# Indexer scores in fewer, fuller visits of tiled products, with five scratch banks and three main banks

## The chip, the cores and the metric

The kernel runs on one core of a Trainium2 chip. The metric is the device time of one execution in microseconds (us), taken as the median of several runs. The engines that matter here are TensorE (PE in the profile, with its weight loads as PEld), VectorE (DVE), ScalarE (ACT), GpSimd (POOL) and SyncE (SP), which issues the DMAs. Products land in PSUM banks; DVE and ACT read them from there.

## The reference, cut to what matters

Two layers act on a prompt of 256 tokens and on eight sample requests of 16 tokens, which the kernel keeps side by side as 384 columns. In each layer, one projection of the normalised input yields queries, keys, values, indexer queries and keys, head weights, gates and the inputs of a convolution and of a pooling branch. The indexer decides which keys each query may attend to:

```python
logits = jnp.einsum('bqhd,bsd->bqhs', qi, ki) * IDX_DIM ** -0.5
score = jnp.einsum('bqhs,bqh->bqs', jax.nn.relu(logits), wi) * N_IDX_HEADS ** -0.5
score = jnp.where(visible[None], score, -jnp.inf)
_, idx = lax.top_k(score, topk)
```

There are 16 indexer heads of width 64. For the prompt, the kernel computes the scores of queries 0 to 63 not at all (all their keys are taken), of queries 64 to 127 over 128 keys, and of queries 128 to 255 over 256 keys; for each sample request it computes them over 144 keys. The rest of a layer is softmax attention over the chosen keys, a depthwise convolution with layer norm, windowed pooling, gates, the output projection, and a gated embedding term.

## The kernel before

**Products of inputs with weights.** `mstep` computes 128 output rows of a projection for all 384 tokens. It takes a bank of PSUM with the tag "mm", runs 16 blocks of depth 128 and, for each, three products in fp32r: high part by high part (L238), low part of the input by high part of the weight (L239), and high by low (L240). That is 48 products with 384 columns, in two halves of 24. The weights come in pieces of eight blocks. SP loads a piece into one of three raw buffers, ACT rounds it to its high part `whi` (L114), and DVE subtracts to get the low part `wlo` (L115). The reading of a finished bank, called its evacuation here, isn't issued at the end of a step: it is put into a queue, and `run_pending` issues it in the middle of the next step.

**Side work.** The indexer, the softmax, the convolution, the pooling and the norm's statistics lie in generators (`att_gen` is that of the attention). After each half step `pump` advances one of them to its next `yield`, so that the side work's products stand between the halves of the main products. They use PSUM banks with the tag "sd". Both tags have four banks of the eight.

**The steps around the change.** The steps of a layer run in the order t0, gb0, ga0, qi0 to qi7, gb1, ga1, v, four pooling steps, k0, k1, gb2, ga2, q0 to q3, gb3, ga3, q4 to q7, and three kinds of gate steps. The step t0 yields the indexer's keys and the head weights. Its evacuation `ev_t0` (L387 to L395) first scales the tables (L347) by the row scale `rb`, and then makes `wiT` (L387, DVE) and the keys (L390 DVE, L391 and L392 ACT, and so on). `rb` comes out of the statistics: small products at L156, a reciprocal and a root (L161 to L166), three transposes on PE (L170), and a copy (L175). The steps qi0 to qi7 leave out the first 64 tokens and so have 320 columns.

**The indexer.** `att_gen` waits until t0 has been evacuated, transposes the head weights (L627) and spreads those of the sample requests (L629). Once the qi steps are done it computes the scores of the first 128 keys and then of all 256 in eight visits each. A visit takes two "sd" banks and has two products (L651), one for each of two heads, which lie in the upper and the lower 64 rows of the array. ACT applies the relu, and DVE weighs each head and adds (L658, L660). `topk` follows (L609 and L612, on DVE). For the sample requests there are eight such pairs (L691), each followed by a weighing on DVE (L696, L698) and a sum over heads on PE (L680). Every product of the indexer in plain fp32 shows as two records, so a pair shows as "x4".

**What sets the order.** The program goes through a scheduling framework that fixes each engine's order of instructions at build time. It places a step when its buffers are free by its own plan, so the number of banks moves instructions.

Of the kernel before, what the change touches and what calls it, by code (L numbers as in the profile page):

```python
# [47 lines left out]
def hybrid_kernel(ctx, tc, I, O):  # L48
# [99 lines left out]
    def bank(tag):  # L148
        return psum.tile([128, 512], F32, name=tag, tag=tag, bufs=4)

# [82 lines left out]
    def run_pending(gate):  # L233
        while pending and gate():
            pending.popleft()()
# [92 lines left out]
    for l in range(DEPTH):  # L328
# [4 lines left out]
        with ExitStack() as mixctx:  # L333
            mix = mixctx.enter_context(tc.tile_pool(name=f"mix{l}", bufs=1))

            def mt(shape, tag, bufs=1, dt=F32, name=None):
                return mix.tile(list(shape), dt, name=name or tag, tag=tag, bufs=bufs)
# [42 lines left out]
            wiT = mt([16, N], "gth", name="wiT")  # L380
            wi_tok = mt([128, 2, 16], "wi_tok")
            wi_s = mt([128, 2, NB], "wi_s")
# [238 lines left out]
            def att_gen():  # L621
                while "t0" not in flags:
                    yield

                ps = bank("sd")
                for i in range(2):
                    T.transpose(ps[:, 16 * i:16 * i + 16], wiT[:, 128 * i:128 * i + 128], ident[0:16, 0:16])  # L627
                for j in range(2):
                    T.matmul(ps[:, 128 + 128 * j:256 + 128 * j], em[0:16, 128 * j:128 * j + 128], wiT[:, TP:],  # L629
                             start=True, stop=True)  # L630
                V.tensor_copy(wi_tok.rearrange("p a b -> p (a b)"), ps[:, 0:32])
                w2 = mt([128, 2, 128], "rp", bufs=2, name="w2")
# [4 lines left out]
                while "qi" not in flags:  # L637
                    yield


                for qt in range(2):
                    nk = 128 * (qt + 1)
                    r = slice(64, 128) if qt == 0 else slice(0, 128)
                    c = slice(0, 64) if qt == 0 else slice(64, 192)
                    acc = mt([128, TP], "sc", bufs=2)[r, :nk]
                    for t in range(8):

                        pss = [bank("sd") for _ in range(2)]
                        for j in range(2):
                            h = slice(64 * j, 64 * j + 64)  # L650
                            T.matmul(pss[j][r, :nk], qi[t][h, c], kiT[h, :nk], start=True, stop=True)  # L651
                        rl = mt([128, 512], "rp", bufs=2, name="rl")[r]
                        for j in range(2):
                            A.activation(rl[:, j * nk:j * nk + nk], pss[j][r, :nk], AF.Relu)
                        for j in range(2):
                            w = wi_tok[r, qt, 2 * t + j:2 * t + j + 1]
                            if t == 0 and j == 0:
                                V.tensor_scalar(acc, rl[:, :nk], w, None, OP.mult)  # L658
                            else:
                                V.scalar_tensor_tensor(acc, rl[:, j * nk:j * nk + nk], w, acc, OP.mult, OP.add)  # L660
                        yield
                    if qt == 0:
                        G.memset(maskp[0][0:64, 0:64], 0.0)
                        G.memset(maskp[0][0:64, 64:128], OFF)
                    else:
                        V.memset(acc[0:64, nk - 64:nk], NEG)
                    yield from topk(acc, 64)
                    V.tensor_scalar(maskp[qt][r], acc, TAKEN, OFF, OP.not_equal, OP.mult)
                    yield

                scp = bank("sd")

                def load_ki(b):
                    kb = mt([128, 2, KS], "kb", bufs=2, name="kib")[:, 0, :]
# [7 lines left out]

                kb = load_ki(0)
                yield
                before = None
                for b in range(NB):
                    nxt = load_ki(b + 1) if b + 1 < NB else None
                    pss = [bank("sd") for _ in range(2)]
                    for j in range(2):
# [4 lines left out]
                    rl = mt([128, 512], "rp", bufs=2, name="rls")  # L694
                    for j in range(2):
                        V.tensor_scalar(rl[:, j * KS:j * KS + KS], pss[j][:, :KS], 0.0,  # L696
                                        wi_s[:, j, b:b + 1], OP.max, OP.mult)
                    V.tensor_tensor(rl[:, :KS], rl[:, :KS], rl[:, KS:2 * KS], OP.add)  # L698
                    before, kb = rl, nxt
                    yield  # L700
                add_s(NB - 1, before)
                flags.add("idx")
# [438 lines left out]
```

## Time and profile before

| what | value |
|---|---|
| median of three runs | 1517.2 us (1515.77 to 1517.27) |
| the profiled execution's own time | 1517.27 us |
| its span, first to last instruction | 1515.4 us |
| PE busy | 1493.7 us, 99% |
| DVE busy | 1000.8 us, 66% |
| ACT busy | 667.1 us, 44% |

The profiled execution took 1.9 us more than its span; that much lies around the first and the last instruction. It is the slowest of the three runs by 0.07 us. PE is busy from the head to the tail of the program. A busy PE says nothing of how well it is used: a visit of small products counts as busy time too, from its drain to the next main product at full pace. The distance between the starts of neighbouring main products shows that pace.

### The profile page before, as it was taken

The page shows a single profiled execution, that of the slowest core. Times are in us where ns is not written, and L with a number is a line of the kernel's source. Part 1 is how long each engine was busy: PE and PEld are TensorE (multiplying, and loading weights), DVE is VectorE, ACT ScalarE, POOL GpSimd, SP SyncE. Part 2 cuts the span into 40 slices and gives each one's busy share as a digit, 9 for nine tenths or more (in the row PEclk, how much of TensorE's full clock was granted, in tenths as well). Part 3 has the DMA queues.
Part 4 walks back from the last instruction along what each step waited for, and adds up shares of the span by engine and source line. Part 5 has one row for each costly group of instructions (what it writes and reads, how often), then busy time and mean ns, then how long its engine had stood idle before and what let it go on. Part 6 is the DMA issues. An engine that isn't in the chain of part 4 may idle for free.

```text
span 1515.4 us, 22769 instructions
## 1 busy us (share of the span) xinstructions
PE 1493.7 (99%) x8839; PEld 1449.6 (96%) x8839; DVE 1000.8 (66%) x1775; ACT 667.1 (44%) x1163; POOL 3.6 (0%) x36
## 2 busy tenths in 40 slices
PE   8999999999999999999999999999999999999995
PEld 8999999999999999999999999999999999999995
DVE  7887979767466444466678797978655654445554
ACT  7653333347543333444445334344554343345441
POOL 0000000000000000000000000000000000000000
PEclk9999999999999999999999999999999999999997
DMA  9654443433446444455454444443344644444432
GB/s 339 207 154 132 149 130 113 137 110 98 135 150 205 126 126 128 132 181 175 152 172 153 134 144 129 127 138 112 98 119 131 201 137 131 128 125 125 126 111 84
DMA packets 84684, 216.10 MB, mean 143 GB/s; under 512 B 11232, under 2 KB 40800, under 8 KB 84576
## 3 DMA queue, kind: packets, MB, share of 16 engines
q1 hardware_dynamic: 84576, 214.65, 45.8%
q8 instruction: 69, 1.13, 0.3%
q14 instruction: 39, 0.32, 0.1%
HBM read 200.70 MB, written 13.91 MB: 142 GB/s over the span
## 4 chain that ended last, share of the span: by engine, by line
PE 98%; DVE 1%; ACT 1%; DMA 0%; SPq 0%; issue 0%; DVEq 0%
PE mm L238 29%; PE mm L240 29%; PE mm L239 29%; PE sd L651 1%; PE sd L238 1%; PE sd L240 1%; PE sd L239 1%; PE mm L851 1%; PE mm L852 1%; PE mm L853 1%; PE sd L715 1%; PE sd L742 1%; PE sd L691 1%; DVE xr L998 0%; DMA wraw<-in_wpp_dram 0%; PE sd L779 0%
## 5 line engine op out<-in xcount | busy, mean ns | idle before, releaser
L114 ACT ACTIVATE whi<-wraw 128x1024 fp32r<-128x1024 f32 (+1 forms) x341 | 357.7, 1050 | 631.6 <-PE mm L239 469.7
L115 DVE TENSOR_TENSOR wlo<-wraw,whi 128x1024 fp32r<-128x1024 f32 (+1 forms) x341 | 412.9, 1211 | 229.6 <-ACT whi L114 227.6
L238 PE MATMUL mm<-xh,whi 128*128 128x384 f32 (+1 forms) x752 | 252.5, 336 | 0.5 <-ACT whi L114 0.5
L238 PE MATMUL mm<-nh,whi 128*128 128x384 f32 (+1 forms) x752 | 252.4, 336 | 0.0
L240 PE MATMUL mm<-nh,wlo 128*128 128x384 f32 (+1 forms) x752 | 250.5, 333 | 0.0
L240 PE MATMUL mm<-xh,wlo 128*128 128x384 f32 (+1 forms) x752 | 250.5, 333 | 0.0
L239 PE MATMUL mm<-nl,whi 128*128 128x384 f32 (+1 forms) x752 | 249.2, 331 | 0.0
L239 PE MATMUL mm<-xl,whi 128*128 128x384 f32 (+1 forms) x752 | 248.9, 331 | 0.0
L238 PE MATMUL mm<-ph,whi 128*128 128x384 f32 x512 | 171.4, 335 | 0.0
L240 PE MATMUL mm<-ph,wlo 128*128 128x384 f32 x512 | 171.0, 334 | 0.0
L239 PE MATMUL mm<-pl,whi 128*128 128x384 f32 x512 | 171.0, 334 | 0.0
L239 PE MATMUL mm<-cl,whi 128*128 128x384 f32 x512 | 171.0, 334 | 0.0
L240 PE MATMUL mm<-ch,wlo 128*128 128x384 f32 x512 | 171.0, 334 | 0.0
L238 PE MATMUL mm<-ch,whi 128*128 128x384 f32 x512 | 170.7, 334 | 0.0
L483 DVE SCALAR_TENSOR_TENSOR ca<-u,cst,ca 128x384 f32<-128x384 f32 x240 | 147.3, 614 | 3.1
L238 PEld LDWEIGHTS mm<-xh,whi 128*128 128x128 f32 x752 | 141.2, 188 | 6.4 <-issue 4.1
L238 PEld LDWEIGHTS mm<-nh,whi 128*128 128x128 f32 x752 | 141.2, 188 | 5.5 <-issue 4.1
L240 PEld LDWEIGHTS mm<-nh,wlo 128*128 128x128 f32 x752 | 141.2, 188 | 1.2 <-issue 0.6
L239 PEld LDWEIGHTS mm<-nl,whi 128*128 128x128 f32 x752 | 141.2, 188 | 1.1 <-issue 0.8
L240 PEld LDWEIGHTS mm<-xh,wlo 128*128 128x128 f32 x752 | 141.2, 188 | 1.2 <-issue 0.6
L239 PEld LDWEIGHTS mm<-xl,whi 128*128 128x128 f32 x752 | 141.2, 188 | 1.0 <-issue 0.8
L239 PEld LDWEIGHTS mm<-pl,whi 128*128 128x128 f32 x512 | 96.1, 188 | 0.0
(221 smaller groups left out, 1850.1 us busy)
## 6 DMA issues: line engine op xcount, KB each, us to landing
wraw<-in_win_dram SPq DMA_DIRECT2D x196, 512.0 KB, 3.7
wraw<-in_wout_dram SPq DMA_DIRECT2D x64, 512.0 KB, 3.6
wraw<-in_wple_dram SPq DMA_DIRECT2D x64, 512.0 KB, 3.6
wraw<-in_wpp_dram SPq DMA_DIRECT2D x7, 512.0 KB, 4.2
x<-in_xT_dram SPq DMA_DIRECT2D x16, 192.0 KB, 5.6
pp_dram<-t SPq DMA_DIRECT2D x16, 192.0 KB, 4.9
xr<-in_xT_dram SPq DMA_DIRECT2D x16, 192.0 KB, 5.8
ppt<-pp_dram SPq DMA_DIRECT2D x16, 192.0 KB, 4.0
```

What stands on the lines that cost most here:

```text
L114: A.activation(hi[:, c], r[:, c], AF.Copy)
L115: V.tensor_tensor(lo[:, c], r[:, c], hi[:, c].bitcast(F32), OP.subtract)
L238: T.matmul(ps, hi_w, hx, start=first, stop=False)
L239: T.matmul(ps, hi_w, lx, start=False, stop=False)
L240: T.matmul(ps, lo_w, hx, start=False, stop=last)
L483: V.scalar_tensor_tensor(av, u[:, :, j:j + 16], w, av, OP.mult, OP.add)
L651: T.matmul(pss[j][r, :nk], qi[t][h, c], kiT[h, :nk], start=True, stop=True)
L691: T.matmul(pss[j][:, :KS], qis[h, b].rearrange("p t j -> p (t j)"), kb[h], start=True, stop=True)
L715: T.matmul(o, q[2 * hp + i][:, 128 * qt:128 * qt + 128], kT[g][:, :nk], start=True, stop=False)
L742: T.matmul(ps.rearrange("p (i c) -> p i c", i=4), Vt[:, kt, 128 * g:128 * g + 128], pt[:, kt], start=(kt == 0), stop=(kt == qt))
L851: T.matmul(outs[i], xh[:, c], wh, start=(k == 0), stop=False, skip_group_check=True)
L852: T.matmul(outs[i], xh[:, c], wl, start=False, stop=False, skip_group_check=True)
```

## The change

Seven things change.

- `bank` gives the tag "mm" three banks and the tag "sd" five.
- The head weights' products in `att_gen` come two yields later.
- The scores of the first 128 keys are computed in two visits of eight products. Each product has a tile of 64 by 64; four tiles stand in the array at a time, in two rows and two columns. Heads of even pairs yield the upper 64 rows of the bank, and heads of odd pairs the lower. So the weighing acts on 128 rows, with weights laid out for that (`wi_2`), and one copy on ACT and one addition on DVE join the halves.
- The scores of all 256 keys are computed in four visits of four products.
- The sample scores are computed in four visits of four products.
- `load_ki` loads the sample keys of two requests before each visit, and not those of one.
- `v_step` calls `run_pending` before it takes its banks.

```diff
-        return psum.tile([128, 512], F32, name=tag, tag=tag, bufs=4)
+        return psum.tile([128, 512], F32, name=tag, tag=tag, bufs=3 if tag == "mm" else 5)
...
                 while "t0" not in flags:
                     yield
+                yield
+                yield
...
-                V.tensor_copy(wi_tok.rearrange("p a b -> p (a b)"), ps[:, 0:32])
+                V.tensor_copy(wi_tok, ps[:, 16:32])
+                for a in range(2):
+                    V.tensor_copy(wi_2[64 * a:64 * a + 64],
+                                  ps[64:128, 0:16].rearrange("p (u a j) -> p u a j", u=4, a=2)[:, :, a])
...
-                    for t in range(8):
-
-                        pss = [bank("sd") for _ in range(2)]
+                nk = 128
+                acc = mt([128, TP], "sc", bufs=2)[:, :nk]
+                for u in (0, 2):
+                    pss = []
+                    for v in (u, u + 1):
+                        ps = [bank("sd") for _ in range(2)]
+                        for a in range(2):
+                            for j in range(2):
+                                h = slice(64 * j, 64 * j + 64)
+                                T.matmul(ps[j][64 * a:64 * a + 64, :nk], qi[2 * v + a][h, 0:64], kiT[h, :nk],
+                                         start=True, stop=True)
+                        pss.append(ps)
+                    for v in (u, u + 1):
+                        weigh(acc, relu(pss[v - u], nk), nk, lambda j: wi_2[:, v, j:j + 1], v == 0)
+                    yield
+                half = mt([128, TP], "sc", bufs=2, name="half")
+                A.activation(half[64:128, :nk], acc[0:64], AF.Copy)
+                acc = acc[64:128]
+                V.tensor_tensor(acc, acc, half[64:128, :nk], OP.add)
...
+                for t in range(0, 8, 2):
+                    pss = []
+                    for i in range(2):
+                        ps = [bank("sd") for _ in range(2)]
                         for j in range(2):
                             h = slice(64 * j, 64 * j + 64)
-                            T.matmul(pss[j][r, :nk], qi[t][h, c], kiT[h, :nk], start=True, stop=True)
+                            T.matmul(ps[j][:, :nk], qi[t + i][h, 64:192], kiT[h, :nk], start=True, stop=True)
+                        pss.append(ps)
+                    for i in range(2):
+                        weigh(acc, relu(pss[i], nk), nk,
+                              lambda j: wi_tok[:, 2 * (t + i) + j:2 * (t + i) + j + 1], t + i == 0)
                     yield
...
-                kb = load_ki(0)
+                kbs = [load_ki(b) for b in range(2)]
                 yield
-                before = None
-                for b in range(NB):
-                    nxt = load_ki(b + 1) if b + 1 < NB else None
-                    pss = [bank("sd") for _ in range(2)]
-                    for j in range(2):
-                        h = slice(64 * j, 64 * j + 64)
-                        T.matmul(pss[j][:, :KS], qis[h, b].rearrange("p t j -> p (t j)"), kb[h], start=True, stop=True)
-                    if before is not None:
-                        add_s(b - 1, before)
+                before = []
+                for b in range(0, NB, 2):
+                    nxt = [load_ki(b + 2 + i) for i in range(2)] if b + 2 < NB else None
+                    pss = []
+                    for i in range(2):
+                        ps = [bank("sd") for _ in range(2)]
+                        for j in range(2):
+                            h = slice(64 * j, 64 * j + 64)
+                            T.matmul(ps[j][:, :KS], qis[h, b + i].rearrange("p t j -> p (t j)"), kbs[i][h], start=True,
+                                     stop=True)
+                        pss.append(ps)
+                    for i, rl in enumerate(before):
+                        add_s(b - 2 + i, rl)
...
             def v_step(gate):
+                run_pending(gate)
                 outs = [bank("mm")[:, 0:256] for _ in range(3)]
```

In the changed kernel the scores' products stand at L671 (first), L694 (second) and L731 (sample), the head weights' products at L630 and L632, and `ev_t0` begins at L388.

**Where instructions move: PE in layer 0, at the end of step ga0 and the start of qi0.** `xh_15` is the last block of ga0; products with 320 columns are qi0's. Before:

```order
235 L238 MATMUL mm<-xh_15_392,whi 128x384
236 L239 MATMUL mm<-xl_15_393,whi 128x384
237 L240 MATMUL mm<-xh_15_392,wlo 128x384
238 L238 MATMUL mm<-xh_0_170,whi 128x320
239 L239 MATMUL mm<-xl_0_171,whi 128x320
```

and now:

```order
235 L238 MATMUL mm<-xh_15_392,whi 128x384
236 L239 MATMUL mm<-xl_15_393,whi 128x384
237 L240 MATMUL mm<-xh_15_392,wlo 128x384
238 L170 MATMUL sd<-cst,st_y 128x128 x3
239 L630 MATMUL sd<-cst,wiT 128x16 x2
240 L632 MATMUL sd<-wiT,em 128x128 x2
241 L238 MATMUL mm<-xh_0_170,whi 128x320
```

The transposes of the row scale, which stood 19 products behind qi0's first, and the head weights' products, which stood behind qi0's last, now stand ahead of qi0's first product.

**DVE at the same place.** `wlo` is a split of a weight piece, `rb` the row scale, `tab` the table, and `st_` names are the statistics. Before:

```order
57 L115 TENSOR_TENSOR wlo<-wraw,whi 128x1024
58 L166 SCALAR_TENSOR_TENSOR st_y<-st_u,st_y 128x3
59 L115 TENSOR_TENSOR wlo<-wraw,whi 128x1024 x2
60 L175 COPY rb<-sd 128x384
61 L347 TENSOR_TENSOR tab_401<-tab_401,rb 128x384 x2
62 L387 SCALAR_TENSOR_TENSOR wiT<-mm,rb 16x384
63 L390 TENSOR_TENSOR t<-mm,tab_401 64x384
```

and now:

```order
56 L166 SCALAR_TENSOR_TENSOR st_y<-st_u,st_y 128x3
57 L115 TENSOR_TENSOR wlo<-wraw,whi 128x1024 x2
58 L175 COPY rb<-sd 128x384
59 L115 TENSOR_TENSOR wlo<-wraw,whi 128x1024
60 L347 TENSOR_TENSOR tab_401<-tab_401,rb 128x384 x2
61 L388 SCALAR_TENSOR_TENSOR wiT<-mm,rb 16x384
62 L391 TENSOR_TENSOR t<-mm,tab_401 64x384
```

The statistics are finished ahead of the splits that stood among them, and one split now stands between `rb` and the tables.

**PE at the first scores of layer 0.** Row 649 and its neighbours are the first visit; the second stands 24 main products further down. Now:

```order
648 L240 MATMUL mm<-xh_7_252,wlo 128x384
649 L671 MATMUL sd<-kiT,qi_0_410 64x128 x2
650 L671 MATMUL sd<-kiT,qi_1_411 64x128 x2
651 L671 MATMUL sd<-kiT,qi_2_412 64x128 x2
652 L671 MATMUL sd<-kiT,qi_3_413 64x128 x2
653 L238 MATMUL mm<-xh_8_310,whi 128x384
```

Eight products stand together where before two stood, with 24 main products to the next two. The second scores and the sample scores stand in the same way, four visits of four products each, in both layers.

## Rows read from the trace of the kernel before

**Rows 1.** Page, parts 1 and 4: engines' busy time; chain that ended last.

```profile
PE 1493.7 (99%) x8839; PEld 1449.6 (96%) x8839; DVE 1000.8 (66%) x1775; ACT 667.1 (44%) x1163; POOL 3.6 (0%) x36
...
PE 98%; DVE 1%; ACT 1%; DMA 0%; SPq 0%; issue 0%; DVEq 0%
```

**Rows 2.** Waits of PE: us in total, times, longest.

```profile
PE sd L238 <- ACT whi L114: 4.5, 2, 4.1
```

**Rows 3.** Timeline of PE, a visit of the second scores: start, us, line, operation.

```profile
176.46 0.34 PE L240 MATMUL mm<-xh,wlo 128*128 128x384 f32 x1
...
178.17 0.34 PE L239 MATMUL mm<-xl,whi 128*128 128x384 f32 x1
```

**Rows 4.** The same, a visit of the first scores.

```profile
112.94 0.34 PE L240 MATMUL mm<-xh,wlo 128*128 128x384 f32 x1
...
114.39 0.34 PE L239 MATMUL mm<-xl,whi 128*128 128x384 f32 x1
```

**Rows 5.** The same, a visit of the sample scores.

```profile
242.25 0.34 PE L240 MATMUL mm<-xh,wlo 128*128 128x384 f32 x1
...
243.78 0.34 PE L239 MATMUL mm<-xl,whi 128*128 128x384 f32 x1
```

**Rows 6.** The same, column tiles in the sample attention.

```profile
395.60 0.47 PE L779 MATMUL sd<-kkb,qas 128*64 128x144 f32 x4
```

**Rows 7.** The same, the first main product, with the idle time before it.

```profile
19.18 0.45 PE L238 MATMUL mm<-xh,whi 128*128 128x384 f32 x1 [0.47 <-ACT whi L114]
```

**Rows 8.** Timeline of PE in layer 0 around the head weights' products.

```profile
51.18 0.33 PE L240 MATMUL mm<-xh,wlo 128*128 128x384 f32 x1
...
54.14 0.49 PE L170 MATMUL sd<-cst,st_y 128*128 128x128 f32 x3
...
58.81 0.29 PE L627 MATMUL sd<-cst,wiT 16*128 16x16 f32 x2
...
59.57 0.42 PE L238 MATMUL mm<-xh,whi 128*128 128x320 f32 x1
```

**Rows 9.** Timeline of DVE at the same place.

```profile
50.53 1.22 DVE L115 TENSOR_TENSOR wlo<-wraw,whi 128x1024 fp32r<-128x1024 f32 x1
...
55.07 0.55 DVE L175 COPY rb<-sd 128x384 f32<-128x384 f32 x1
...
56.72 0.55 DVE L387 SCALAR_TENSOR_TENSOR wiT<-mm,rb 16x384 f32<-16x384 f32 x1
```

**Rows 10.** Timeline of ACT at the same place.

```profile
58.38 0.48 ACT L392 ACTIVATE t<-mm 32x384 f32<-32x384 f32 x1
```

**Rows 11.** Timeline of PE at the head, as the matmuls quicken.

```profile
5.52 0.69 PE L238 MATMUL sd<-phi,whi 128*128 128x384 f32 x1 [0.41 <-ACT whi L114]
...
10.48 0.52 PE L240 MATMUL sd<-phi,wlo 128*128 128x384 f32 x1
...
11.28 0.33 PE L239 MATMUL sd<-plo,whi 128*128 128x384 f32 x1
```

**Rows 12.** Windows: busy us (count) of each engine, granted clock, DMA share, GB/s.

```profile
160.00:180.00 20.00, 20.00 (x116) 19.42 (x116) 19.20 (x47) 6.91 (x9) 0.39 (x4) 1.00 0.52 157
...
1496.40:1499.20 2.80, 0.00 (x0) 0.00 (x0) 1.67 (x3) 0.96 (x2) 0.00 (x0) 1.00 0.00 0
1499.30:1515.40 16.10, 2.35 (x9) 1.86 (x9) 8.90 (x22) 2.10 (x3) 0.00 (x0) 0.50 0.53 195
```

**Rows 13.** Groups of DVE, 100 to 290 us: busy us, mean ns, idle.

```profile
L115 DVE TENSOR_TENSOR wlo<-wraw,whi 128x1024 fp32r<-128x1024 f32 (+1 forms) x42 | 50.7, 1208 | 14.1 <-ACT whi L114 13.8
L483 DVE SCALAR_TENSOR_TENSOR ca<-u,cst,ca 128x384 f32<-128x384 f32 x72 | 44.2, 614 | 1.0
L660 DVE SCALAR_TENSOR_TENSOR sc<-rl,wi_tok,sc 64x128 f32<-64x128 f32 (+1 forms) x30 | 12.5, 416 | 2.0 <-ACT rl L654 1.0
```

**Rows 14.** Timeline of DVE, the eighth gate product read from its bank.

```profile
438.99 0.55 DVE L574 SCALAR_TENSOR_TENSOR t<-mm,rb 128x384 f32<-128x384 f32 x1
```

**Rows 15.** Timeline of PE, the third step after that product begins.

```profile
431.60 0.42 PE L238 MATMUL mm<-xh,whi 128*128 128x384 f32 x1
```

More of the change, by code (lines that the diff above doesn't have):

```diff
@@ L638, in att_gen, with relu @@
                     yield
[L641 to L645, printed above, removed]
-                    for t in range(8):
-                        pss = [bank("sd") for _ in range(2)]
+                def relu(ps, nk):
+                    rl = mt([128, 512], "rp", bufs=2, name="rl")
+                    for j in range(2):
+                        A.activation(rl[:, j * nk:j * nk + nk], ps[j][:, :nk], AF.Relu)
+                    return rl
@@ new lines, in weigh @@
+                def weigh(acc, rl, nk, w, first):
+                    for j in range(2):
+                        if first and j == 0:
+                            V.tensor_scalar(acc, rl[:, :nk], w(j), None, OP.mult)
+                        else:
+                            V.scalar_tensor_tensor(acc, rl[:, j * nk:j * nk + nk], w(j), acc, OP.mult, OP.add)
+                nk = 128
[5 more added lines that the diff above has]
+                        for a in range(2):
+                            for j in range(2):
+                                h = slice(64 * j, 64 * j + 64)
[5 more added lines that the diff above has]
+                    yield
@@ new lines, in att_gen @@
+                half = mt([128, TP], "sc", bufs=2, name="half")
+                A.activation(half[64:128, :nk], acc[0:64], AF.Copy)
+                acc = acc[64:128]
+                V.tensor_tensor(acc, acc, half[64:128, :nk], OP.add)
+                G.memset(maskp[0][0:64, 0:64], 0.0)
+                G.memset(maskp[0][0:64, 64:128], OFF)
+                yield from topk(acc, 64)
+                V.tensor_scalar(maskp[0][64:128], acc, TAKEN, OFF, OP.not_equal, OP.mult)
+                nk = 256
@@ L649, in att_gen @@
+                acc = mt([128, TP], "sc", bufs=2)
+                for t in range(0, 8, 2):
+                    pss = []
+                    for i in range(2):
+                        ps = [bank("sd") for _ in range(2)]
                         for j in range(2):
                             h = slice(64 * j, 64 * j + 64)
-                            T.matmul(pss[j][r, :nk], qi[t][h, c], kiT[h, :nk], start=True, stop=True)
-                        rl = mt([128, 512], "rp", bufs=2, name="rl")[r]
@@ L653, in att_gen @@
-                        for j in range(2):
[L654 to L660, printed above, removed]
@@ L669, in att_gen @@
+                        pss.append(ps)
+                    for i in range(2):
+                        weigh(acc, relu(pss[i], nk), nk,
+                              lambda j: wi_tok[:, 2 * (t + i) + j:2 * (t + i) + j + 1], t + i == 0)
                     yield
+                V.memset(acc[0:64, nk - 64:nk], NEG)
+                yield from topk(acc, 64)
+                V.tensor_scalar(maskp[1], acc, TAKEN, OFF, OP.not_equal, OP.mult)
+                yield
                 scp = bank("sd")
+                pair = []
@@ L673, in load_ki @@
                 def load_ki(b):
-                    kb = mt([128, 2, KS], "kb", bufs=2, name="kib")[:, 0, :]
+                    if b % 2 == 0:
+                        pair.append(mt([128, 2, KS], "kb", bufs=2, name="kib"))
+                    kb = pair[-1][:, b % 2, :]
                     S.dma_start(out=kb[:, :PAST], in_=I["ckiT"][l, b])
@@ new lines, in att_gen @@
+                for b in range(0, NB, 2):
[3 more added lines that the diff above has]
+                        ps = [bank("sd") for _ in range(2)]
+                        for j in range(2):
+                            h = slice(64 * j, 64 * j + 64)
[4 more added lines that the diff above has]
+                        add_s(b - 2 + i, rl)
+                    before = []
+                    for i in range(2):
+                        rl = mt([128, 512], "rp", bufs=2, name="rls")
+                        for j in range(2):
+                            V.tensor_scalar(rl[:, j * KS:j * KS + KS], pss[i][j][:, :KS], 0.0,
+                                            wi_s[:, j, b + i:b + i + 1], OP.max, OP.mult)
+                        V.tensor_tensor(rl[:, :KS], rl[:, :KS], rl[:, KS:2 * KS], OP.add)
+                        before.append(rl)
+                    kbs = nxt
@@ L700, in att_gen @@
                     yield
-                add_s(NB - 1, before)
+                for i, rl in enumerate(before):
+                    add_s(NB - 2 + i, rl)
                 flags.add("idx")
```

18 lines of the change are left out of this document (2 added, 16 removed).

## The prediction

> **What bounds the kernel now.** I read the page first: PE is busy for 1493.7 us, 99% of the span, and the chain that ended last is PE for 98% [rows 1]. PE's waits come next: the largest is 4.5 us on the first weight pieces at the head [rows 2], and none stands in the middle. So time is gained only where PE's own sequence gets shorter, and lost where PE begins to wait. The timeline shows how it gets shorter. Main products start 0.173 us apart (24 in a half step, 4.16 us). Around a visit of indexer products they don't: from the last main product ahead of a visit of the second scores to the fifth one behind it 1.71 us pass [rows 3], where five times 0.173, 0.87, would do. The visit costs 0.85.
>
> **The visits.** The same reading gives 1.45 − 0.87 = 0.58 for a visit of the first scores [rows 4], and 1.53 − 0.87 = 0.66 for one of the sample scores [rows 5]. A visit's price has a fixed part, which is leaving and re-entering the main products' full tiles, and a part that grows with columns. Second and sample visits differ in that alone: 256 against 144 columns, 0.85 against 0.66, so 0.0017 us a column, or 0.43 for a pair with 256 columns, 0.24 with 144, 0.21 with 128. A pair added to a visit should cost that alone.
>
> Second scores: eight visits, 6.8 a layer, become four of 0.85 + 0.43 = 1.28, 5.1 together. Saved: 1.7.
>
> Sample scores: eight pairs in ten visits (two pairs are split by a main product) cost 6.6 over the layer; four visits of 0.66 + 0.24 = 0.90 cost 3.6. Saved: 3.0. The sums over heads (L680) stay eight.
>
> First scores: eight visits cost 4.6; two visits remain. If the two columns of tiles work together, as the two rows do, eight products are two rounds: 0.58 + 0.21 = 0.80 each, 1.6 together. Saved: 3.0. The nearest row on column tiles is the sample attention's: four records of 0.31 us each lie within 0.47 us [rows 6], so I take them as working together. If they did not, two more rounds a visit would cost 0.43 and the saving would be 2.1.
>
> That is 7.7 a layer and **15.3** in both; bounds 13.5 and 15.5. The copy and the addition for the halves lie on ACT and DVE behind other work, and PE doesn't wait for the mask before the softmax, tens of us later. The larger key loads wait on nothing that PE needs soon: the first is issued well ahead of the visits.
>
> **The head.** With a fifth scratch bank, six more products of the embedding term run ahead of the first main product, where PE idles 0.47 us and starts at 19.18 [rows 7]. They took six times 0.173 later on. The idle time is filled and a little of the approach with it: **0.6** gained, bounds 0 and 1.0.
>
> **The stall in layer 0.** This is what speaks against the change. With four main banks, qi0, the fourth step, takes a fresh one. With three it takes t0's, which `ev_t0` must have read, and that needs `rb`. So the transposes (L170), the head weights' products and qi0 now stand behind ga0's last product, in the order that the section on the change shows. PE has finished that product at about 51.35 before [rows 8], now about 50.7 by the head's gain, and the transposes last to 51.25. On DVE the statistics are finished early now, two splits end by about 51.3, and `rb` starts there. Before, `rb` started at 55.07 [rows 9] and the last read of t0's bank, the second copy on ACT, ended at 58.38 + 0.48 = 58.86 [rows 10]: 3.8 us. Now one split more (1.14, from a split's start to its follower's) stands between. So t0's bank comes free at about 51.35 + 1.14 + 3.8 = 56.3. Without the wait, qi0 would begin at 51.25 + 0.76 (head weights' products, 58.81 to 59.57 [rows 8]) = 52.0. **Lost: 4.2.** The head weights' products run inside that wait, from about 54.85 (`wiT` ends 2.2 us behind `rb`'s start [rows 9], and the split). Bounds: 3, if DVE's splits stand closer, and 5, if a weight piece is late. Layer 1 has no such place: its `rb` is made long before.
>
> **The clock.** PE is idle here from 51.25 to 54.85, 3.6 us, and again for 0.7. At the end of the program the granted clock still reads 1.00 (2.4 GHz) through 2.8 us without a product, and 0.50 (1.2 GHz) from 1499.3 on [rows 12], 2.9 us after the last one. At the head, work resumed at 5.52, records last 0.52 until 10.48 and 0.33 from 11.28 [rows 11]. So the clock may fall in this stall, and some 5.5 us of work would then run at half pace: 2.8 lost. If it doesn't fall, nothing is. I take **1.2**, since 3.6 is only just beyond 2.9 and the head weights' products come within it.
>
> **DVE.** The sample visits move some 45 us earlier, into a stretch where DVE is busy 19.20 of 20 us [rows 12]. Between the first weighing of the second scores and the second sample sum, DVE's order now holds 100 instructions. Nine splits at 1.208, 14 convolution taps at 0.614, and 15 weighings at 0.416 [rows 13] are 25.7; the other 62 (pooling windows, top-k, embedding) come to 24.9 by the same view, 50.6 in all. By starts rather than ends, since each row begins some 0.04 before its forerunner has ended, it is 46.4. PE has 240 main products there, 41.6, and visits of 4 × 1.28 + 0.9: 47.7. Between no wait and 2.9 per layer, I take 0.8, because 46.4 is nearer to what a full DVE does: **1.6** in both layers.
>
> **The sum.** 15.3 + 0.6 − 4.2 − 1.2 − 1.6 = 8.9. From the profiled execution's 1517.27 (its span of 1515.4 and 1.9 around it; the median is 1517.2) that gives **1508.4**. `v_step`'s earlier `run_pending` and its third bank cost nothing in this sum: that bank's first product stands 24 products of 0.12, 2.9 us, behind the step's first, and the evacuation that it waits for is two DVE reads of 0.55 each. If DVE were late there, up to 1 us a layer would be lost; that is within the range.
>
> **The rivals.**
>
> *The clock falls and DVE waits at its bound*: 2.8 in place of 1.2 and 3.6 in place of 1.6, so 5.3 gained: about 1512. For it: 3.6 is longer than 2.9. Chance 0.15.
>
> *The stall isn't there, or half*: DVE's splits are quicker out of the way, or qi0's start hides. 8.9 + 4.2 gives 1504.2 with the clock kept up at 1503.0. Against it: the order fixes the chain, `rb` to the last read is 3.8 by rows. Chance 0.12.
>
> *Evacuation becomes the bound*: visits of four products fill four of five scratch banks, the next visit needs three of them read out, and DVE's 50.6 against 47.7 holds for the second scores and, with the same rows, again for the sample visits: 2.9 twice a layer is 11.6 and not 1.6 in both. No waits before speak for it; full slices do. 8.9 + 1.6 − 11.6 leaves the time within 0.2%: about 1518. Chance 0.11. Beside this stands a rule that speaks against the change: the Trainium skill's page TensorEngine Tiling (Array Packing), section PSUM Bottleneck, says that tiling speeds TensorE and not the evacuation of PSUM, so that the copies out of PSUM may become the bottleneck. The trace agrees in so far as DVE is 96% busy in that stretch [rows 12]; by the rule the time would be this rival's, by the rows of waits the forecast's.
>
> *Slower: three main banks are too few at the gates.* A step's bank is needed again three steps later. The eighth gate read ends at 438.99 + 0.55 = 439.54 [rows 14] on a bank whose product was finished at the end of its step, and the third step after begins at 431.60 [rows 15]. With three banks PE would wait 7.9 us there, 15.9 in both layers: 1508.4 + 15.9 = 1524.3. It decides as soon as DVE's order doesn't bring that read earlier by 7.9. In the changed order 99 splits of weights stand ahead of it and not 101: one step of 48 products, 8.3 us, earlier. So the planner has moved it just enough, and DVE isn't full there. Chance 0.07.
>
> *The change doesn't do what it says* (the framework splits the new visits again) is excluded by the order: the visits stand together in both layers.
>
> **How the numbers follow.** Forecast, 1506 to 1511: 0.55. The rivals: 0.15, 0.12, 0.11, 0.07. The range is to hold 8 in 10: down to 1503, where the stall is missing, and up to 1514, where clock and DVE are at their bounds and the stall is 5 (15.3 + 0.6 − 5 − 2.8 − 5 = 3.1: 1514.2); the last two rivals are left out. A difference of 0.2%, 3.0 us, is about what a measurement of this kernel can tell from no change: below 1514.2 is faster. Faster: 0.55 + 0.15 + 0.12 = 0.82; same: 0.11; slower: 0.07.
>
> **What would show it.** In the changed profile: visits at L694 of 1.28, at L731 of 0.90, and at L671 of 0.80 by the same reading; L671 at 1.2 would mean that column tiles take turns. PE's waits should name DVE's `wiT` for about 3.6 us and an ACT or DVE read for about 0.7 near 51 to 56 us, with main products 0.32 apart behind them if the clock fell. Waits of PE on reads of "sd" between 160 and 260 us measure the DVE term; waits on reads of "mm" between 400 and 440 us would be the slower rival. The forecast is wrong if a pair added to a visit costs as much as a visit, or if qi0 begins by 53 us.

## The result, and the profile after

The changed kernel takes 1506.07 us (median of four runs, 1505.98 to 1506.55), the kernel before 1516.75 in the runs that stand beside it (1515.77 to 1517.27). The ratio is 0.9931, with a 95% interval of 0.9914 to 0.9948: 10.7 us faster. The forecast was 1508.4, with a range of 1503 to 1514. The profiled execution took 1505.98 with a span of 1503.7, and the rows below are from it.

The page's part 1 and PE's waits of the changed kernel (waits: us in total, times, longest), for [rows 1, 2]:

```profile
PE 1478.8 (98%) x8839; PEld 1448.7 (96%) x8839; DVE 996.3 (66%) x1765; ACT 661.5 (44%) x1149; POOL 3.6 (0%) x36
```

```profile
PE sd L238 <- ACT whi L114: 4.5, 2, 4.1
...
PE sd L630 <- DVE wiT L388: 3.3, 1, 3.3
...
PE mm L238 <- ACT t L393: 0.8, 1, 0.8
```

PE is busy for 14.9 us less and waits for two things that it didn't wait for: `wiT` (3.3) and ACT's copy out of t0's bank (0.8). Both are the stall in layer 0. No wait on DVE or ACT stands between 60 us and the tail.

**The visits.** PE's timeline, a visit of the first scores, of the second scores and of the sample scores, for [rows 3 to 5]; in each, the last row is the fifth main product behind the visit:

```profile
117.53 0.34 PE L240 MATMUL mm<-xh,wlo 128*128 128x384 f32 x1
117.80 0.67 PE L671 MATMUL sd<-kiT,qi 64*64 64x128 f32 x16
...
119.21 0.34 PE L239 MATMUL mm<-xl,whi 128*128 128x384 f32 x1
```

```profile
154.34 0.34 PE L240 MATMUL mm<-xh,wlo 128*128 128x384 f32 x1
154.61 1.14 PE L694 MATMUL sd<-kiT,qi 64*128 64x256 f32 x8
...
156.49 0.33 PE L239 MATMUL mm<-xl,whi 128*128 128x384 f32 x1
```

```profile
196.53 0.34 PE L240 MATMUL mm<-xh,wlo 128*128 128x384 f32 x1
196.80 0.76 PE L731 MATMUL sd<-kib,qis 64*128 64x144 f32 x8
...
198.30 0.33 PE L239 MATMUL mm<-xl,whi 128*128 128x384 f32 x1
```

By the prediction's reading, less 5 × 0.173 = 0.87, the visits cost 1.68 − 0.87 = 0.81, 2.15 − 0.87 = 1.28, and 1.77 − 0.87 = 0.90. The forecast was 0.80, 1.28 and 0.90.

**The stall and the clock.** PE's timeline behind step ga0, for [rows 8]:

```profile
50.28 0.34 PE L240 MATMUL mm<-xh,wlo 128*128 128x384 f32 x1
50.45 0.49 PE L170 MATMUL sd<-cst,st_y 128*128 128x128 f32 x3
54.24 0.29 PE L630 MATMUL sd<-cst,wiT 16*128 16x16 f32 x2 [3.30 <-DVE wiT L388]
...
55.83 0.63 PE L238 MATMUL mm<-xh,whi 128*128 128x320 f32 x1 [0.75 <-ACT t L393]
...
58.39 0.44 PE L238 MATMUL mm<-xh,whi 128*128 128x320 f32 x1
58.66 0.32 PE L239 MATMUL mm<-xl,whi 128*128 128x320 f32 x1
```

The last product of ga0 starts 0.9 earlier than before. The transposes follow, then 3.3 us without work, the head weights' products, and 0.75 without work again. Then qi0 begins, with products 0.27 apart up to 58.39 and 0.15 apart from 58.66. Windows over the same place (busy us and count of PE, PEld, DVE, ACT and POOL, then the granted clock, DMA share, GB/s), for [rows 12]:

```profile
50.90:54.20 3.30, 0.04 (x1) 0.00 (x0) 3.18 (x5) 1.06 (x1) 0.00 (x0) 1.00 0.96 314
55.10:55.80 0.70, 0.00 (x0) 0.00 (x0) 0.70 (x1) 0.66 (x2) 0.00 (x0) 0.61 0.53 217
55.80:58.40 2.60, 2.57 (x10) 2.57 (x11) 2.43 (x9) 1.81 (x2) 0.00 (x0) 0.50 0.44 153
58.70:60.00 1.30, 1.30 (x11) 1.30 (x11) 1.28 (x4) 0.99 (x3) 0.00 (x0) 1.00 0.28 104
```

The granted clock is 1.00 (2.4 GHz) while PE waits for `wiT`, 0.61 as a mean over the second wait, 0.50 (1.2 GHz) for the first ten products of qi0, and 1.00 from then on. DVE's timeline shows what PE waits for, for [rows 9]:

```profile
50.98 0.56 DVE L175 COPY rb<-sd 128x384 f32<-128x384 f32 x1 [0.65 <-PE sd L170]
51.45 1.22 DVE L115 TENSOR_TENSOR wlo<-wraw,whi 128x1024 fp32r<-128x1024 f32 x1
...
53.64 0.55 DVE L388 SCALAR_TENSOR_TENSOR wiT<-mm,rb 16x384 f32<-16x384 f32 x1
```

`rb` starts at 50.98, right behind the transposes; the split of a weight piece (1.14 to its follower) stands between it and the tables, and `wiT` begins at 53.64. That is the chain that the prediction read off the order, but for its start: DVE had its two splits done and stood idle for 0.65 us until the transposes were there, where the prediction had `rb` wait for the splits until 51.3.

**Where the rest came.** The six products of the second norm's statistics (L156) mark a place late in layer 0. They start at 626.77 in the kernel before and at 623.49 now:

```profile
626.77 0.72 PE L156 MATMUL sd<-ones,ss 128*128 128x1 f32 x6
```

```profile
623.49 0.72 PE L156 MATMUL sd<-ones,ss 128*128 128x1 f32 x6
```

So layer 0 up to there gained 3.3. The last main product starts at 1496.05 before and here at 1484.83:

```profile
1484.83 0.34 PE L240 MATMUL mm<-ph,wlo 128*128 128x384 f32 x1
```

That is 11.2 in all, and so 7.9 in the rest, which holds layer 1's indexer and no stall.

### The profile page after: what moved, and what is told of

Its sections match the earlier page's. It is cut to its first block, busy times and chain, and to the rows that moved or that the text cites. A ratio compares the mean times of both kernels' runs of the same rounds, so it can differ in the third digit from the quotient of the medians.

```text
span 1503.7 us, 22743 instructions
## 1 busy us (share of the span) xinstructions
PE 1478.8 (98%) x8839; PEld 1448.7 (96%) x8839; DVE 996.3 (66%) x1765; ACT 661.5 (44%) x1149; POOL 3.6 (0%) x36
## 4 chain that ended last, share of the span: by engine, by line
PE 98%; DVE 1%; DMA 0%; ACT 0%; issue 0%; SPq 0%; DVEq 0%
PE mm L238 29%; PE mm L240 29%; PE mm L239 29%; PE sd L238 1%; PE sd L240 1%; PE sd L239 1%; PE mm L899 1%; PE mm L900 1%; PE mm L898 1%; PE sd L761 1%; PE sd L788 1%; PE sd L694 1%; DVE xr L1045 0%; PE sd L825 0%; PE sd L851 0%; PE sd L731 0%
## 5 line engine op out<-in xcount | busy, mean ns | idle before, releaser
L238 PEld LDWEIGHTS mm<-ph,whi 128*128 128x128 f32 x512 | 96.1, 188 | 0.0
```

Of the source, the lines that this page charges most:

```text
L238: T.matmul(ps, hi_w, hx, start=first, stop=False)
```

## The experiments

Each kernel is compared with the changed kernel's 1506.07, its own runs being taken beside runs of the kernel before (1517.0 to 1517.3 in median, up to 0.5 above those beside the changed kernel, so that differences of that size mean nothing here). Three theories were tried first: that the stall comes from the banks, that its slow products are the clock's, and that DVE has little room.

**banks_only.** The kernel before with the banks alone.

```diff
-        return psum.tile([128, 512], F32, name=tag, tag=tag, bufs=4)
+        return psum.tile([128, 512], F32, name=tag, tag=tag, bufs=3 if tag == "mm" else 5)
...
             def v_step(gate):
+                run_pending(gate)
```

> The kernel before with three main and five scratch banks (and the call of run_pending that v_step then needs), old visits and old place of the head weights' products in the code. Theory: the banks alone make the stall in layer 0, since qi0 takes t0's bank: PE waits 3.3 us for wiT and 0.75 for ACT, the clock falls for some 10 products (1.2), and the head gives 0.9 back, so 4.2 to 4.6 us slower than before, about 1521.2. Rival (the stall comes from the two yields): about 1516, no wait at the head weights. Second rival (three main banks are short at the gates): waits on reads of mm between 400 and 440 us, 1524 or more.

Measured: 1532.52 (1528.45 to 1535.31), ratio to the kernel before 1.0101 (1.0086 to 1.0115). Its waits of PE:

```profile
PE mm L238 <- DVE mxs L784: 3.9, 6, 0.7
...
PE sd L627 <- DVE wiT L387: 2.3, 1, 2.3
PE mm L238 <- ACT t L392: 2.0, 1, 2.0
PE sd L805 <- ACT t L798: 1.7, 4, 0.4
PE mm L238 <- DVE t L574: 1.6, 2, 0.8
```

The theory and the second rival hold together, and the price is larger than either. The stall is there with the old visits and without the yields (`wiT` 2.3, ACT 2.0). And the prediction's slower rival is there as well: PE waits in the gates' stretch, between 364 and 432 us and again in layer 1, for 3.9 + 1.7 + 1.6 = 7.2 us. The prediction looked for such waits, priced them at 7.9 a layer, and gave them a chance of 0.07. In the changed kernel none of them stands.

**late16.** So something in the change takes them away. Counted in main products, the softmax of the first heads begins 120 products earlier in the changed kernel than in banks_only, and the sample attention 53 earlier, because the indexer ends earlier. This kernel moves the softmax back by 144, 24 past its place in banks_only; the sample attention then begins at the same product as in banks_only. The visits stay as full as in the change.

```diff
                 flags.add("idx")
+                for _ in range(16):
+                    yield
```

> The changed kernel with 16 yields more in the attention's generator behind the sample scores, so that the softmax of the first heads begins some 145 products later, at the place that it has in banks_only; the visits stay as full as in the change. Theory: the waits of banks_only between 390 and 445 us (4.8 us a layer, three main banks short at the gate steps) are gone in the change only because its indexer ends early enough for the softmax to begin when its queries are there; with the yields they return, 9.6 us slower than the changed kernel, about 1515.7. Rival (they belong to the old visits): 1506 to 1507, no wait of PE on reads of mm.

Measured: 1517.94 (1514.79 to 1521.21), and 1515.6 in the profiled execution. Its waits of PE:

```profile
PE mm L238 <- DVE mxs L832: 3.9, 6, 0.7
...
PE sd L853 <- ACT t L846: 1.7, 4, 0.4
PE mm L238 <- DVE t L575: 1.6, 2, 0.8
```

The three groups of waits are those of banks_only to the tenth: 3.9, 1.7 and 1.6. In the group of 1.7, products of the sample attention wait for their own operands. The other two, 5.5 us, are waits for a main bank. The name `mxs`, the maximum in a sample's softmax, misleads there, as DVE and PE show at one of them:

```profile
412.21 0.55 DVE L575 SCALAR_TENSOR_TENSOR t<-mm,rb 128x384 f32<-128x384 f32 x1
412.68 0.14 DVE L832 TENSOR_SCALAR mxs<-mxs 128x1 f32<-128x1 f32 x1
```

```profile
412.82 0.44 PE L238 MATMUL mm<-xh,whi 128*128 128x384 f32 x1 [0.67 <-DVE mxs L832]
```

L575 reads a gate product out of its main bank and ends at 412.76, 0.06 ahead of PE's next step; `mxs` merely stands behind it and touches no main bank. The span is 1513.3 against 1503.7, 9.6 longer, as expected; the median is 2.2 above the expected 1515.7. So the waits belong to three main banks with the sample attention at its old place, and not to the old visits. The fuller visits pay twice: by their own price, and by ending the indexer early enough that three main banks do. A part of them is enough for the second: sample_pairs and second_pairs below have none of these waits.

The waits make up 7.2 of the 9.6, and the other 2.4 stand at the same places. The visit at 409.68, for one, takes 413.62 − 409.51 − 0.87 = 3.24, of which 1.09 are its two waits; the same products cost 0.89 + 0.45 + 0.45 = 1.79 in the changed kernel, and 0.36 is left. Four such places come to 1.2 in a layer, and to 2.4 in both.

The executions of these two kernels lie up to 7 us apart, where those of the changed kernel lie within 0.6. The mean granted clock goes with them: in late16 it is 0.993 to 0.994 in the four of 1514.8 to 1515.6, 0.992 in the three of 1517.7 to 1518.3, and 0.990 in the four of 1520.4 to 1521.2; in banks_only 0.994 at 1528.5, 0.992 at 1530.8 and 1532.5, and 0.990 at 1535.0 and 1535.3. A mean that is lower by 0.004 over 1513 us is 12 us more at half the clock, and so about 6 us lost; that is an estimate from these numbers, and it is the spread. Where in the program the clock was down for longer isn't shown, since the profiled executions are of the shorter kind.

**filler.** 18 products that nothing reads, in the stall.

```diff
+                if l == 0:
+                    ps = bank("sd")
+                    for i in range(18):
+                        T.matmul(ps[:, :N], xs[0][0][:, 0:128], xs[0][0], start=(i == 0), stop=(i == 17))
                 ps = bank("sd")
```

> The changed kernel with 18 products of 384 columns that nothing reads, on a scratch bank of their own, between the transposes and the head weights' products of layer 0: they fill PE's wait of 3.3 us with 3.1 us of work. Theory: the half pace of the ten products behind the wait is the granted clock's fall during the wait; with PE kept at work they run 0.147 apart and not 0.267, so 1.2 us faster than the changed kernel, about 1504.9. Rival (these products are slow because DVE or the weight loads are late): they stay 0.267 apart, 1506.1.

Measured: 1504.63 (1504.43 to 1506.93), 1.4 faster than the changed kernel with more work. Its timeline at the place:

```profile
50.79 3.40 PE L631 MATMUL sd<-xh 128*128 128x384 f32 x18
...
55.92 0.41 PE L238 MATMUL mm<-xh,whi 128*128 128x320 f32 x1 [0.76 <-ACT t L393]
56.17 0.31 PE L239 MATMUL mm<-xl,whi 128*128 128x320 f32 x1
56.32 0.31 PE L240 MATMUL mm<-xh,wlo 128*128 128x320 f32 x1
```

qi0 begins at 55.92, as late as in the changed kernel and behind the same short wait (0.76), but from its second product on the products are 0.15 apart, and the granted clock reads 1.00 throughout. So the half pace was the granted clock's answer to the long wait; DVE and the weight loads have no part in it.

**t0_copy.** The bank of t0 is copied to SBUF at once, in layer 0 (`early` is set for that step alone).

```diff
+        if early:
+            raw = tmp()
+            A.activation(raw, ps[:, :N], AF.Copy)
+            ps = raw
         pending.append(lambda: evac(ps))
...
```

> The changed kernel with t0's bank of layer 0 copied by ACT into SBUF as soon as its products are done; what ev_t0 read from the bank it reads from that copy. Theory: qi0 then has a free bank and the planner puts the head weights' products behind qi0; the waits of 3.3 and 0.75 and the slow products go, 5.1 us faster than the changed kernel less at most 0.5 for the copy: 1501 to 1501.5. Rival (what DVE does late is late for PE at the next step anyway, a wait at qi1 on gb0's or ga0's bank): a wait of 2 to 4 us about 8 us later, 1504 to 1506.

Measured: 1501.03 (1500.74 to 1501.42), ratio 0.9894 (0.9880 to 0.9907). Windows over the place:

```profile
50.00:60.00 10.00, 10.00 (x70) 9.64 (x69) 9.25 (x18) 5.98 (x7) 0.00 (x0) 1.00 0.67 211
```

PE doesn't wait and the clock stays at 1.00. The kernel is 5.0 us faster than the changed one; its last main product starts at 1479.47 and not at 1484.83, 5.4 earlier, which is what the stall (4.1) and its clock (1.3) cost the changed kernel. The copy takes ACT 0.49 us and PE waits for nothing behind it.

**dve_load.** Eight reductions more a layer on DVE, beside the weighing of the second scores.

```diff
+    junk = const.tile([128, 1], F32, name="junk")
...
                 def weigh(acc, rl, nk, w, first):
+                    if nk == 256:
+                        V.tensor_reduce(junk, rl, axis=AX, op=OP.max)
```

> The changed kernel with eight reductions more on DVE per layer, one beside each weighing of the second scores (512 columns, about 0.6 us each, 4.8 us a layer), that nothing reads. Theory of the prediction's DVE term (46.4 us of DVE against 47.7 of PE, a margin of 1.3 per layer): PE waits about 3.5 us a layer, about 7 us slower than the changed kernel, 1513. Rival (the queue behind gives way, since what stands there is needed much later): no wait of PE above 0.5, at most 0.5 us a layer for a visit that is split, 1506 to 1507.

Measured: 1508.86 (1507.70 to 1509.26). The reductions took 0.675 each, 5.4 us a layer; in layer 0 they lie between 153 and 177 us. No wait of PE is added; its span is 1.8 longer, and 0.84 a layer of that is a visit that the planner split. Windows of the changed kernel and then of this one:

```profile
160.00:180.00 20.00, 20.00 (x118) 18.95 (x118) 19.45 (x43) 7.87 (x14) 0.39 (x4) 1.00 0.40 129
180.00:200.00 20.00, 20.00 (x124) 19.21 (x123) 19.97 (x58) 7.57 (x14) 0.11 (x1) 1.00 0.53 164
```

```profile
160.00:180.00 20.00, 20.00 (x114) 18.40 (x114) 20.00 (x40) 7.13 (x14) 0.11 (x1) 1.00 0.36 108
```

DVE is busy for 19.97 of 20 us in a window of the one and for all 20 in a window of the other, and PE waits for it in neither kernel. So the rival is right on the waits: the queue gives way, and work moves back behind the reductions, where PE doesn't need it yet (from 200 to 220 us DVE is busy for 15.78 and not for 13.19). Its time, 1506 to 1507, was missed. Two executions lie at 1507.7, at a mean granted clock of 0.994 and 0.995, and three at 1508.9 to 1509.3, at 0.992; so the clock goes with the longer ones here too.

**one_column.** The first scores in the upper 64 columns of the array alone.

```diff
-                                T.matmul(ps[j][64 * a:64 * a + 64, :nk], qi[2 * v + a][h, 0:64], kiT[h, :nk],
-                                         start=True, stop=True)
+                            T.matmul(pss[2 * (v // 2) + j][64:128, nk * (v % 2):nk * (v % 2) + nk], qi[u + v][h, 0:64],
+                                     kiT[h, :nk], start=True, stop=True)
...
```

> The changed kernel with the first scores in one column of tiles: visits of up to eight products, all of them in the upper 64 columns of the array, so four rounds of two row tiles where the change has two rounds of four tiles. Theory (column tiles work together): a visit of eight products costs 0.58 + 3 x 0.21 = 1.22 and not 0.81; the planner splits the second visit in six and two, so 1.2 + 1.05 + 0.45 = 2.7 and not 1.62: 1.1 us a layer, 2.2 slower than the changed kernel, 1508.3. Rival (column tiles take turns): the visit of eight costs 0.81 as before, 0.6 a layer for the split alone, 1507.3.

Measured: 1510.66 (1510.62 to 1511.36). Its first visit, eight products again:

```profile
119.09 0.34 PE L240 MATMUL mm<-xh,wlo 128*128 128x384 f32 x1
119.36 1.09 PE L667 MATMUL sd<-kiT,qi 64*64 64x128 f32 x16
...
121.19 0.35 PE L239 MATMUL mm<-xl,whi 128*128 128x384 f32 x1
```

2.10 − 0.87 = 1.23, where four tiles at a time took 0.81: column tiles work together, and the theory's 1.22 is met. The kernel is 4.6 slower (5.4 in the profiled execution) and not 2.2, for three reasons that the theory left out. The visits of six and of two products cost 1.24 and 0.79, and not 1.05 and 0.45: in the trace the last two of the six, and the two left over, start one by one, 0.11 us from record to record, where the records of a pair start together. That fits products of one bank, which in this kernel lie in the same rows of the array. The planner also split a sample visit in each layer; with both, a layer lost 2.1. And in layer 0 the clock stayed low after the stall for longer, with main products 0.27 apart up to some 62 us, 1.4 more.

**no_yields.** The change without the two yields.

```diff
                 while "t0" not in flags:
                     yield
-                yield
-                yield
```

> The changed kernel without the two yields ahead of the head weights' products. Theory: in layer 0 their place is set by the banks, not by the yields (the order is the same there), and in layer 1 PE waits for nothing there either way: within 0.5 us of the changed kernel, 1506. Rival (the yields keep TensorE from waiting for wiT in layer 1): a wait at the head weights' products near 770 us, 1 to 2 us slower.

Measured: 1506.22 (1505.74 to 1506.97). The later place of the head weights' products in the code does nothing by itself: in layer 0 the banks set it. Of the seven changes, two were not measured alone: the larger key loads went back only together with the sample visits, and `v_step`'s earlier `run_pending` was tried only together with the banks.

**sample_pairs and second_pairs.** One part of the visits back at a pair each.

```diff
-                for b in range(0, NB, 2):
-                    nxt = [load_ki(b + 2 + i) for i in range(2)] if b + 2 < NB else None
+                for b in range(NB):
+                    nxt = load_ki(b + 1) if b + 1 < NB else None
...
```

> The changed kernel with the sample scores alone back at one pair a visit: eight visits, which the planner here leaves whole, where the change has four. Theory: 8 x 0.66 = 5.3 and not 3.5, 1.8 a layer, 3.6 slower than the changed kernel, 1509.7; the waits at the gate steps stay away, since the softmax begins within 8 products of its place in the change. Rival (the ten visits of before were dear only because of what stood beside them): less than 1 us slower.

Measured: 1510.78 (1509.32 to 1511.14).

```diff
-                for t in range(0, 8, 2):
+                for t in range(8):
...
```

> The changed kernel with the second scores alone back at one pair a visit, eight visits and not four. Theory: 8 x 0.85 = 6.8 and not 5.1, 1.7 a layer, 3.4 slower than the changed kernel, 1509.5. Rival (fuller visits give back on DVE what they save on PE): within 1 us of the changed kernel.

Measured: 1510.15 (1509.22 to 1510.53). They are 4.7 and 4.1 slower than the changed kernel, and not 3.6 and 3.4. The difference is the clock again, as windows of sample_pairs and then of second_pairs show (columns as above):

```profile
60.00:61.50 1.50, 1.50 (x7) 1.50 (x7) 1.43 (x3) 0.21 (x2) 0.00 (x0) 0.50 0.38 87
```

```profile
58.00:60.00 2.00, 2.00 (x10) 2.00 (x9) 1.87 (x5) 1.36 (x4) 0.00 (x0) 0.50 0.53 205
60.00:62.00 2.00, 2.00 (x11) 2.00 (x11) 1.87 (x5) 1.09 (x6) 0.00 (x0) 0.62 0.53 151
```

In both the clock reads 0.50 up to about 61.5 and not to 58.4, behind waits of 2.3 and 2.0 in sample_pairs and of 3.3 and 0.2 in second_pairs, where the changed kernel has 3.3 and 0.8. By the starts of PE's products, the stall and its clock cost 1.7 and 1.1 us more than in the changed kernel. The spans are 5.5 and 4.5 longer, so 3.8 and 3.4 are left, against 3.6 and 3.4 expected; the visits cost 0.65 and 0.85 a pair in these profiles.

**best.** t0_copy, and fuller visits still: up to four products share a bank (shown for the second scores).

```diff
-                    for i in range(2):
-                        ps = [bank("sd") for _ in range(2)]
+                    full = [bank("sd") for _ in range(4)]
+                    for i in range(4):
+                        ps = [full[2 * (i // 2) + j][:, nk * (i % 2):nk * (i % 2) + nk] for j in range(2)]
...
```

> t0_copy, and two products of 256 columns, or up to four of 128, side by side in one scratch bank: the first scores in one visit of sixteen products, the second in two of eight, the sample scores in four of four on two banks. Theory (an added pair costs its columns alone): first 0.58 + 3 x 0.21 = 1.22 and not 1.62, second 2 x (0.85 + 3 x 0.43) = 4.28 and not 5.11, sample as in the change, 1.2 us a layer: 2.4 faster than t0_copy's 1501.0, 1498.6. Rival (bursts of twice the evacuation hold PE up): waits of PE behind the visits, 1501 or more.

Measured: 1497.85 (1496.92 to 1498.82), ratio to the kernel before 0.9874 (0.9859 to 0.9889). It beats both kernels, by 19.3 and 8.2 us. Its visit of sixteen first products, four rounds of four tiles, and the waits of PE:

```profile
111.58 0.34 PE L240 MATMUL mm<-xh,wlo 128*128 128x384 f32 x1
111.85 1.10 PE L676 MATMUL sd<-kiT,qi 64*64 64x128 f32 x32
...
113.69 0.33 PE L239 MATMUL mm<-xl,whi 128*128 128x384 f32 x1
```

```profile
PE sd L238 <- ACT whi L114: 4.1, 1, 4.1
PE sd L156 <- DVE ss L200: 3.5, 1, 3.5
PE sd L170 <- DVE st_y L166: 1.3, 1, 1.3
```

2.11 − 0.87 = 1.24, the price of one_column's eight products in four rounds (1.23). The first of these waits is the head's, the other two are the tail's; the stall has gone. The kernel is 3.2 faster than t0_copy and not 2.4; 0.6 of the other 0.8 lies ahead of 50 us, where the edit changes nothing: the transposes of layer 0 start at 49.99 and not at 50.58.

## Why the prediction was right

**The bound.** PE's own sequence was the bound and stayed so; each term could be read on it.

**The visits (15.3 forecast).** They cost 0.81, 1.28 and 0.90, with 0.80, 1.28 and 0.90 forecast. Layer 1, which has no stall, gained 7.9, with 7.7 forecast; twice that is 15.8. The rule behind it, that an added pair costs its columns alone, was read from two kinds of visits and held for visits of four, eight and sixteen products; in one_column it failed for products that the planner had parted from their partners. The assumption on column tiles, taken from one row, is shown by one_column.

**The head (0.6).** 0.9: the last product of ga0 starts at 50.28 and not at 51.18 [rows 8]. The six products of the embedding term, 1.04 at full pace, do run ahead now; the first main product starts only 0.11 later for it, at 19.29 and not at 19.18 [rows 7], and without a wait. The size is loose: over the profiles of all kernels here with five scratch banks, what follows ga0 starts between 49.99 and 50.94, and in the kernel before at 51.36.

**The stall (4.2).** Behind the transposes, qi0 would have started at 50.45 + 0.49 + 0.76 = 51.7; it started at 55.83: 4.1. t0_copy and banks_only show that the banks make it.

**The clock (1.2, between 0 and 2.8).** Ten products took 58.66 − 55.83 = 2.83 and not 1.47; 0.1 of the difference is the return from the small products, which costs that in the kernel before too, so 1.3 was lost. They stood 0.27 apart and not the 0.32 that the prediction named, which is the half pace of 384 columns and not of 320. The value was hit by luck rather than by knowledge: behind the same wait one_column lost 2.7.

**DVE (1.6).** This is the term that failed. It was read as if DVE's queue had to be worked off as PE reaches its own end of the stretch. The order mixes urgent weighings with convolution and pooling that PE needs much later, so a full DVE isn't a late DVE. PE waited for nothing, and dve_load put 5.4 us more a layer on it without a wait. The Trainium skill's page TensorEngine Tiling (Array Packing), section PSUM Bottleneck, says that reading PSUM out may become the bottleneck when tiling makes TensorE faster. In this case's traces it didn't: with DVE busy for 19.97 of 20 us, PE waited for no read of a bank there, and the third rival failed with it.

**The sum.** 15.8 + 0.9 − 4.1 − 1.3 = 11.3 by terms, with layer 1's gain taken for both layers, and 11.2 at the last main product. The tail gave 0.5 more, which no step foretold, so the span is 11.7 shorter. Around the span 2.3 us lie now and not 1.9, so the profiled executions differ by 11.3, and the medians by 10.7. The forecast of 8.9 was short of this by about the DVE term, which didn't come.

**The slower rival (0.07).** It was the right worry. The mechanism is real: with it late16 is 9.6 us longer, 5.5 of it waits for main banks, where the prediction's price was 15.9, and it is part of what makes banks_only 15 us slower than the kernel before. The reason that the prediction gave against it, that the planner places the gate reads a step earlier, is right too. What it did not see is why: the reads move because the indexer ends sooner, as late16 shows, so the safety hangs on the fuller visits and not on the planner's care.

## What to carry to other kernels

About half or more of the price of a pair of short products among long ones is the way in and out (some 0.4 of 0.58 to 0.85 us here): measure one visit, split the price into its fixed and its per-column part by two sizes, and put into a visit as many products as the banks hold, side by side in a bank where they fit. Where a bank is taken from a pool, follow who must read it before it comes round again; a copy to SBUF that costs ACT half a microsecond freed PE of a stall of 5 us here. Check after such a change that the order elsewhere still suits the smaller pool: here three banks were enough only because other work had moved. And a full engine is a bound only if what stands in its queue is needed soon: look at who waits, and not at the busy share.

## What was new of the hardware

After a wait of some 3.3 and 0.75 us, with 0.85 us of small products between, the granted clock went from 1.00 to 0.50 and stayed there for 10 main products in the changed kernel, and for some 22 in one_column, behind the same waits to the tenth: 1.3 against 2.7 us. 18 products that fill the long wait keep it at 1.00, though the short one stays (0.76). So one profiled execution doesn't give the price of such a stall. Four tiles of 64 by 64 in two rows and two columns work together in plain fp32: sixteen products of 128 columns take as long (1.24, best) as eight in two row tiles alone (1.23, one_column).
